# Six gate blocks of the last branch computed in pairs with seven products, and up products as the filler of the forgetting attention

## The chip, the cores and the metric

The kernel runs on one core of a Trainium2 chip. The metric is the device time of one execution in microseconds (us). Before the change the median of three runs is 2095.1 us (2092.2 to 2098.84).

## The reference, cut to what matters

One decoder layer in float32 on a sequence of 1024 tokens with 1024 channels. Its first part, the token mixers, is the one that the change touches:

```python
p = x @ w_in                                   # 1024 x 1024 times 1024 x (mixers + 4*1024 gates)
u_rw  = rwkv7_branch(...) @ rw_up              # each branch: 1024 x 256 times 256 x 1024
u_cv  = conv_branch(...)  @ cv_up
u_gla = gla_branch(...)   @ gla_up
u_fox = fox_branch(...)   @ fox_up             # forgetting attention, 4 heads of 64
gates = sigmoid(p_gate.reshape(B, T, 4, D) + gate_b)
merged = gates[0]*u_rw + gates[1]*u_cv + gates[2]*u_gla + gates[3]*u_fox
x = layer_norm(ALPHA * x + merged @ w_out)     # then cross-attention and a SwiGLU FFN
```

The gates are 4 x 1024 columns of `w_in`, so 32 blocks of 128 columns, 8 for each branch. All values are kept to float32 accuracy.

## The kernel before, in words

Activations lie transposed, channels on the 128 partitions and tokens along the free axis, in two halves of 512 tokens. To keep float32 accuracy every operand is split into a high and a low part (`split`, L161 a cast on ScalarE, L162 a subtraction on VectorE), and one product of 128 channels is three matmuls of 128x128 by 128x512: high times high (L179), high times low (L182), low times high (L183). TensorE therefore does three matmuls for each 128-channel slice (`mm3`).

A block of 128 columns of `w_in` can be computed in two ways. `project` does it directly: two halves of tokens, 8 slices, 3 matmuls, so 48 matmuls a block and 96 for two. The class `Sevens` takes a pair of blocks and the two token halves as a 2x2 matrix of matrices and computes it with seven products of half the depth instead of eight (the Strassen-Winograd scheme): 7 x 4 x 3 = 84 matmuls for two blocks. Its price is sums of weight quarters on GpSimd (`comb`, L389), seven pieces to split for a pair (ScalarE and VectorE), and sums of the outputs on VectorE (L379 to L382 and in `done`, L495).

The stages of the first part, with their places in the trace (us from the start of the span):

1. First projections, 30 to 262: the mixers' blocks. From 70 on they go through `Sevens`: two pairs of the RWKV branch and, from 112 on, eight pairs listed in `pairs0` (L409). `done` adds the last term, applies a sigmoid where one is due, and stores the block to DRAM (L506).
2. RWKV, 262 to about 610. `weave` alternates one step of the branch with pieces of a filler, here `gate_projections`: 16 gate blocks of branches 1 and 2 by `project`, cut in quarters of 6 matmuls, each half stored to `gate_d` in DRAM (L853).
3. Convolution and gated linear attention, then forgetting attention (`fox`, about 720 to 897). The filler is now `merge`: first `first_branch` (8 gate blocks of branch 0, kept on the chip, and its up products), then the 8 gate blocks of the last branch, with `other_branches` between them. `fox` has two head pairs, p = 0 and p = 1, each of 16 units of growing width (128 to 1024 columns, two units of each), and a step of it is followed by two pieces of filler (`FOX_PIECES`), each 6 matmuls whether it is a quarter of a gate block or an up product.
4. What is left of `merge` (`drain(pieces)`), 897 to 1006, and then the output projection.

One unit of `fox` is a chain over three engines: scores on TensorE (`ps_fs`), row maximum on VectorE (L1103, L1105, L1106), exponential on ScalarE (L1109), sum, reciprocal and scaling on VectorE (L1111 to L1113, `fp`), transposes on TensorE (`ps_ft`, L1120), a copy on ScalarE (`fpt`), and the products with the values on TensorE (`ps_fo`, L1133). Three units are in flight.

One up product in `other_branches` is 6 matmuls into `ps_up`, then a multiplication with the gate on VectorE (L1263, `gsig`, which also frees the PSUM bank), then an addition into `merged` on GpSimd (L1264). The gate's half is loaded from `gate_d` on the DMA queue of SyncE (L1252) into a ring of three tiles while the attention runs, and of nine afterwards. For each two up products 128x256 of weights are loaded and split (`uraw`, `uh`, `ul`), and for each branch its values (`yld`, `yh`, `yl`). The PSUM ring of up products and gate quarters has two banks.

Each engine takes its instructions in a fixed order. The order is made when the program is built: a scheduler places the instructions of the branch steps and of the filler, so the places in the code decide it only roughly.

Of the kernel before, what the change touches and what calls it, by code (L numbers as in the profile page):

```python
# [11 lines left out]
F32 = mybir.dt.float32  # L12
# [3 lines left out]
AF = mybir.ActivationFunctionType  # L16
# [6 lines left out]
P = 128  # L23
T = 1024
D = 1024
KD = D // P
# [11 lines left out]
ST_BLOCKS = ["cb0", "ca0", "cb1", "ca1", "gq", "gk", "gv0", "gv1", "gr0", "gr1",  # L38
             "fq0", "fk0", "fv0", "fq1", "fk1", "fv1"]
BLOCKS = RW_BLOCKS + ST_BLOCKS  # L40
# [52 lines left out]
def hybrid_kernel(ctx, tc, io, out):  # L93
    nc = tc.nc
# [4 lines left out]
    act = nc.scalar.activation  # L99
# [6 lines left out]
    stg = ctx.enter_context(tc.tile_pool(name="stg", bufs=3))  # L106
# [3 lines left out]
    dp = ctx.enter_context(tc.tile_pool(name="dp", bufs=1, space=DRAM))  # L110
# [25 lines left out]
    def pc(name, i=0):  # L136
        return par[:, PC[name] + i:PC[name] + i + 1]
# [54 lines left out]
    def drain(gen, n=None):  # L192

        while n is None or n > 0:
            if next(gen, gen) is gen:
                return
            n = n if n is None else n - 1
# [79 lines left out]
    def hs(hf):  # L277
        return slice(hf * TH, (hf + 1) * TH)
# [20 lines left out]
    def project(src, evac, w=None, pieces=1, both=True):  # L299

        wh, wl = w or weight(src)
        for hf in range(2):
            ps = gps("ps_g", both=both)
            pairs = [(wh[:, k * P:(k + 1) * P], wl[:, k * P:(k + 1) * P],
                      xh[k][:, hs(hf)], xl[k][:, hs(hf)]) for k in range(KD)]
            n = KD // pieces
            for i in range(pieces):
                mm3(ps, pairs[i * n:(i + 1) * n], i == 0, i == pieces - 1, lag=2 if pieces == 1 else 99)
                if i == pieces - 1:
                    evac(hf, ps)  # L310
                yield
# [29 lines left out]

    HK = KD // 2

    class Sevens:


# [59 lines left out]

    with ExitStack() as es:
        xtp = es.enter_context(tc.tile_pool(name="xtp", bufs=12))
        pairs0 = list(range(4, 8, 2)) + list(range(9, 9 + len(ST_BLOCKS), 2))  # L409

        def rows(u):
            pool, tag = (pM, "M") if u % 2 else (wp, "raw")
# [67 lines left out]
        for b in pairs0[0:2]:  # L480
            raws = [pM.tile([P, T], F32, tag="M", name="praw") for _ in range(2)]

            def done(i, l, a, ps):
                tt(out=raws[i][:, hs(l)], in0=a, in1=ps, op=ALU.add)
# [4 lines left out]
        for b in pairs0[2:]:  # L489
            held = {}  # L490

            def done(i, l, a, ps):
                n = BLOCKS[b + i]
                t = pM.tile([P, TH], F32, tag="M", name="stg2")
                tt(out=t, in0=a, in1=ps, op=ALU.add)  # L495
                if n[0] == "c":
                    if n[1] == "b":
                        act(t, t, AF.Sigmoid)
                    held.setdefault(l, []).append(t)
                    if len(held[l]) < 2:  # L500
                        return
                    tt(out=t, in0=t, in1=held[l][0], op=ALU.mult)
                    n = "cu" + n[2]
                elif n[:2] == "fq":
                    act(t, t, AF.Copy, scale=0.125)
                nc.sync.dma_start(st_d[n][:, hs(l)], t)  # L506

            sv.seven(rhs0, bank0, term, done)
        for k in range(HK):
            t = pM.tile([P, TH], F32, tag="M", name="x12")  # L510
# [333 lines left out]
        drain(fill)  # L844


    gate_d = dp.tile([24, P, T], F32, tag="gate_d", name="gate_d")

    def gate_block(i, pool, tag):
        def evac(hf, ps):  # L850
            t = pool.tile([P, TH], F32, tag=tag, name="gsig")
            act(t, ps, AF.Sigmoid, bias=pc("gateb", 8 + i))
            nc.sync.dma_start(gate_d[i, :, hs(hf)], t)  # L853

        return project(io["wblk"][len(BLOCKS) + 8 + i], evac, pieces=4, both=False)
# [335 lines left out]
    def values(br, t2):  # L1191

        yh, yl = [], []
        for k in range(2):
            h = t2.tile([P, T], F32R, tag="yh", name="yh", bufs=2)
            l = t2.tile([P, T], F32R, tag="yl", name="yl", bufs=2)
            for hf in range(2):
                t = t2.tile([P, TH], F32, tag="yld", name="yld")
                nc.sync.dma_start(t, y_d[br][k, :, hs(hf)])
                split(h[:, hs(hf)], l[:, hs(hf)], t)  # L1200
            yh.append(h)
            yl.append(l)
        return yh, yl

    def up_weights(br, j, t2):
        raw = t2.tile([P, 256], F32, tag="uraw", name="uraw")
        nc.sync.dma_start(raw, io["ups"][br, j])
        uh = t2.tile([P, 256], F32R, tag="uh", name="uh")
        ul = t2.tile([P, 256], F32R, tag="ul", name="ul")
        split(uh, ul, raw)  # L1210
        return uh, ul
# [26 lines left out]
    def other_branches(t2):  # L1238

        for br in (1, 2, 3):  # L1240
            while br not in ready:
                yield None
            y = values(br, t2)
            us, todo, sgs = [up_weights(br, 0, t2)], [(j, hf) for j in range(KD) for hf in range(2)], []

            def ahead(n):
                while len(sgs) < min(n, len(todo)):
                    j, hf = todo[len(sgs)]
                    late = 3 in ready
                    t = (pB if late else t2).tile([P, TH], F32, tag="B" if late else "sg", name="gsig",  # L1250
                                                  bufs=9 if late else 3)
                    nc.sync.dma_start(t, gate_d[8 * br + j - 8, :, hs(hf)])  # L1252
                    sgs.append(t)

            ahead(2)
            yield None
            for n, (j, hf) in enumerate(todo):
                if hf == 0 and j + 1 < KD:
                    us.append(up_weights(br, j + 1, t2))
                pu = gps("ps_up", both=False)  # L1260
                up_product(pu, us[j], y, hf)
                sg, mj = sgs[n], merged[j][:, hs(hf)]
                tt(out=sg, in0=sg, in1=pu, op=ALU.mult)  # L1263
                nc.gpsimd.tensor_tensor(out=mj, in0=mj, in1=sg, op=ALU.add)  # L1264
                ahead(n + (5 if 3 in ready else 3))
                yield True

    def merge(t2):
        yield from first_branch(t2)
        others = other_branches(t2)  # L1270
        for j in range(KD):
            yield from gate_block(16 + j, stg, "stg")
            for _ in range(10 if 3 in ready else 4):
                if next(others, None) is None:
                    break
                yield
        while True:
            r = next(others, others)
            if r is others:
                return  # L1280
            yield

    ready = {0}
    with ExitStack() as es:
# [569 lines left out]
    for f in reversed(range(LEAD)):  # L1854
        g = lead_up(f, 1, w13[f] if f > 1 else ffn_weights(f), (2, 2))
# [8 lines left out]
    for k in range(HK):  # L1864
        t = diff(x2[k + HK][:, hs(0)], xt[0].h[k + HK].bitcast(F32))
# [203 lines left out]
```

## Time and profile before

| what | us |
|---|---|
| median of three runs (lowest, highest) | 2095.1 (2092.2, 2098.84) |
| the profiled execution, its own time | 2095.68 |
| its span, first to last instruction | 2093.9 |
| first projections through `Sevens`, from the third pair on | 112 to 262 |
| forgetting attention, second head pair (p = 1) | 811 to 897 |
| rest of the merge | 897 to 1006 |

The page gives for each engine its busy time. TensorE is busy for 98% of the span and the chain of work that ended last runs over it for 88%. A matmul of 128x512 shows as 389 ns, but matmuls overlap: a new one starts every 0.226 to 0.227 us, so the count of matmuls in a stretch tells more than their busy time. What costs time besides the number of matmuls is a stretch in which the matmuls start further apart, because TensorE's next one waits for another engine.

### The profile page before, as it was taken

The page shows a single profiled execution, that of the slowest core. Times are in us where ns is not written, and L with a number is a line of the kernel's source. Part 1 is how long each engine was busy: PE and PEld are TensorE (multiplying, and loading weights), DVE is VectorE, ACT ScalarE, POOL GpSimd, SP SyncE. Part 2 cuts the span into 40 slices and gives each one's busy share as a digit, 9 for nine tenths or more (in the row PEclk, how much of TensorE's full clock was granted, in tenths as well). Part 3 has the DMA queues.
Part 4 walks back from the last instruction along what each step waited for, and adds up shares of the span by engine and source line. Part 5 has one row for each costly group of instructions (what it writes and reads, how often), then busy time and mean ns, then how long its engine had stood idle before and what let it go on. Part 6 is the DMA issues. An engine that isn't in the chain of part 4 may idle for free.

```text
span 2093.9 us, 29285 instructions
## 1 busy us (share of the span) xinstructions
PE 2050.9 (98%) x11404; PEld 1673.4 (80%) x11404; DVE 1292.9 (62%) x2237; ACT 768.0 (37%) x1320; POOL 431.9 (21%) x324
## 2 busy tenths in 40 slices
PE   8999999999999999999999999999999999999997
PEld 6888877877777877778788888877888888888877
DVE  8865456398624554654677345677666666666666
ACT  4332254222247567522244233453232222322331
POOL 4332200000000000244124000147131111222343
PEclk9999999999999999999999999999999999999998
DMA  5223242232223203354543102321311211211112
GB/s 169 72 86 106 97 142 87 74 91 68 69 96 99 78 30 121 98 193 139 170 150 124 44 31 81 110 102 41 101 41 41 81 41 41 71 51 41 56 46 81
DMA packets 100506, 181.08 MB, mean 86 GB/s; under 512 B 21030, under 2 KB 45400, under 8 KB 100368
## 3 DMA queue, kind: packets, MB, share of 16 engines
q1 hardware_dynamic: 100368, 179.21, 26.6%
q8 instruction: 90, 1.47, 0.3%
q14 instruction: 48, 0.39, 0.1%
HBM read 141.84 MB, written 37.34 MB: 86 GB/s over the span
## 4 chain that ended last, share of the span: by engine, by line
PE 88%; DVE 3%; POOL 3%; DMA 2%; ACT 2%; issue 2%; SPq 0%; DVEq 0%; POOLq 0%; ACTq 0%
PE ps_w L183 9%; PE ps_w L182 9%; PE ps_w L179 9%; PE ps_g L179 8%; PE ps_g L183 8%; PE ps_g L182 8%; PE ps_q L182 3%; PE ps_q L183 3%; PE ps_q L179 2%; PE ps_gate L179 1%; PE ps_wo L182 1%; PE ps_wo L183 1%; PE ps_wo L179 1%; PE ps_gate L183 1%; PE ps_up L179 1%
## 5 line engine op out<-in xcount | busy, mean ns | idle before, releaser
L182 PE MATMUL ps_g<-xh,wlo 128*128 128x512 f32 x464 | 184.5, 398 | 2.7 <-DVE wlo L162 2.7
L183 PE MATMUL ps_g<-xl,whi 128*128 128x512 f32 x464 | 184.9, 398 | 0.0
L179 PE MATMUL ps_g<-xh,whi 128*128 128x512 f32 x464 | 160.1, 417 | 2.2 <-ACT xh L161 2.2
L161 ACT CAST piece<-wraw 128x512 fp32r<-128x512 f32 x132 | 81.2, 622 | 199.7 <-PE ps_w L183 159.8
L183 PE MATMUL ps_w<-hid,piece 128*128 128x512 f32 (+1 forms) x400 | 143.3, 366 | 2.3 <-DVE hid L162 2.3
L161 ACT CAST piece<-wcomb 128x512 fp32r<-128x512 f32 x112 | 68.5, 621 | 209.5 <-PE ps_w L183 133.4
L182 PE MATMUL ps_w<-hid,piece 128*128 128x512 f32 (+1 forms) x400 | 143.2, 365 | 0.0
L162 DVE TENSOR_TENSOR wlo<-wraw,whi 128x1024 fp32r<-128x1024 f32 x79 | 98.4, 1249 | 58.5 <-ACT whi L161 58.3
L389 POOL TENSOR_TENSOR wcomb<-wraw,wcomb 128x512 f32<-128x512 f32 x28 | 40.8, 1458 | 398.7 <-DVE piece L162 397.7
L1788 DVE TENSOR_TENSOR x<-x,ps_w 128x512 f32<-128x512 f32 x120 | 82.5, 688 | 65.3 <-PE ps_w L183 65.3
L161 ACT CAST whi<-wraw 128x1024 fp32r<-128x1024 f32 x97 | 100.8, 1048 | 57.8 <-issue 18.4
L162 DVE TENSOR_TENSOR piece<-wraw,piece 128x512 fp32r<-128x512 f32 x124 | 96.7, 782 | 34.8 <-ACT piece L161 34.1
L162 POOL TENSOR_TENSOR wlo<-wraw,whi 128x1024 fp32r<-128x1024 f32 x18 | 46.6, 2594 | 321.3 <-ACT whi L161 311.4
L183 PE MATMUL ps_w<-xT,piece 128*128 128x512 f32 x288 | 112.0, 389 | 0.0
L182 PE MATMUL ps_w<-xT,piece 128*128 128x512 f32 x288 | 112.0, 389 | 0.0
L179 PE MATMUL ps_w<-hid,piece 128*128 128x512 f32 (+1 forms) x400 | 108.5, 366 | 0.2 <-DVE x L1786 0.2
L182 PEld LDWEIGHTS ps_g<-xh,wlo 128*128 128x128 f32 x464 | 88.6, 191 | 22.7 <-DVE wlo L162 3.1
L183 PEld LDWEIGHTS ps_g<-xl,whi 128*128 128x128 f32 x464 | 88.7, 191 | 19.8 <-issue 0.8
L179 PEld LDWEIGHTS ps_g<-xh,whi 128*128 128x128 f32 x464 | 83.4, 192 | 25.9 <-ACT xh L161 4.7
L389 POOL TENSOR_TENSOR wcomb<-wraw 128x512 f32<-128x512 f32 x58 | 78.4, 1352 | 101.2 <-DMA wraw<-ffn_w 46.8
L1264 POOL TENSOR_TENSOR merged<-merged,gsig 128x512 f32<-128x512 f32 x48 | 70.0, 1484 | 141.2 <-DVE gsig L1263 89.3
L162 DVE TENSOR_TENSOR piece<-wcomb,piece 128x512 fp32r<-128x512 f32 x112 | 87.3, 786 | 11.0 <-ACT piece L161 10.4
(528 smaller groups left out, 5234.9 us busy)
## 6 DMA issues: line engine op xcount, KB each, us to landing
wraw<-ffn_w SPq DMA_DIRECT2D x72, 512.0 KB
wraw<-wblk SPq DMA_DIRECT2D x57, 512.0 KB
gate_d<-gsig SPq DMA_DIRECT2D x48, 256.0 KB
gsig<-gate_d SPq DMA_DIRECT2D x48, 256.0 KB
wraw<-xa_wo SPq DMA_DIRECT2D x16, 512.0 KB
xraw<-xT SPq DMA_DIRECT2D x16, 256.0 KB
yld<-y_d SPq DMA_DIRECT2D x16, 256.0 KB
uraw<-ups SPq DMA_DIRECT2D x32, 128.0 KB
```

Source lines behind the costliest of these rows:

```text
L161: nc.scalar.copy(hi, src)
L162: eng.tensor_tensor(out=lo, in0=src, in1=hi.bitcast(F32), op=ALU.subtract)
L179: mm(ps, lhsT=pairs[i][0], rhs=pairs[i][2], start=start and i == 0, stop=False)
L182: mm(ps, lhsT=ll, rhs=rh, start=False, stop=False)
L183: latest[0] = mm(ps, lhsT=lh, rhs=rl, start=False, stop=stop and i == n + min(lag, n) - 1)
L389: nc.gpsimd.tensor_tensor(out=t, in0=a, in1=b, op=op)
L1264: nc.gpsimd.tensor_tensor(out=mj, in0=mj, in1=sg, op=ALU.add)
L1788: tt(out=xs, in0=xs, in1=ps, op=ALU.add)
```

## The change

Three edits, and one that follows from them.

- `pairs0` gets three more pairs: the first 6 of the 8 gate blocks of the last branch (`EARLY = 6`) are computed as pairs in the first projections. `done` adds the bias and the sigmoid for them and stores them to `gate_d`, whose allocation moves up for that.
- `merge` no longer interleaves 8 gate blocks with `other_branches`. It takes the steps of `other_branches` one after the other and, where that has nothing to give (it yields `None`) or the attention has ended (`3 in ready`), also a piece of `rest`, the last 2 gate blocks.
- `other_branches` yields `None` six times instead of once before the last branch's up products, and twice before those of the two others.

```diff
+    EARLY = 6
+    gate_d = dp.tile([24, P, T], F32, tag="gate_d", name="gate_d")
...
-        pairs0 = list(range(4, 8, 2)) + list(range(9, 9 + len(ST_BLOCKS), 2))
+        pairs0 = (list(range(4, 8, 2)) + list(range(9, 9 + len(ST_BLOCKS), 2))
+                  + list(range(len(BLOCKS) + 24, len(BLOCKS) + 24 + EARLY, 2)))
...
             def done(i, l, a, ps):
-                n = BLOCKS[b + i]
                 t = pM.tile([P, TH], F32, tag="M", name="stg2")
                 tt(out=t, in0=a, in1=ps, op=ALU.add)
+                g = b + i - len(BLOCKS)
+                if g >= 0:
+                    act(t, t, AF.Sigmoid, bias=pc("gateb", g))
+                    nc.sync.dma_start(gate_d[g - 8, :, hs(l)], t)
+                    return
+                n = BLOCKS[b + i]
...
             ahead(2)
-            yield None
+            for _ in range(6 if br == 3 else 2):
+                yield None
...
         others = other_branches(t2)
-        for j in range(KD):
-            yield from gate_block(16 + j, stg, "stg")
-            for _ in range(10 if 3 in ready else 4):
-                if next(others, None) is None:
-                    break
-                yield
+        rest = itertools.chain(*(gate_block(16 + j, stg, "stg") for j in range(EARLY, KD)))
         while True:
             r = next(others, others)
             if r is others:
-                return
-            yield
+                break
+            if r is None or 3 in ready:
+                if r:
+                    yield
+                next(rest, None)
+            yield
+        drain(rest)
```

How the instructions move is shown at two places, both in the forgetting attention at p = 1, at the units that are 768 columns wide. On TensorE, in the kernel before, the transposes of one unit, the scores of the next and what stands after them (`ps_g` is a gate block's bank):

```order
L1120 MATMUL ps_ft<-cst,fp 128x128 x6
L179 MATMUL ps_fs<-fkh,fqh 128x512
L182 MATMUL ps_fs<-fkh,fq 128x512
L183 MATMUL ps_fs<-fk,fqh 128x512
L179 MATMUL ps_fs<-fkh,fqh 128x256
L182 MATMUL ps_fs<-fkh,fq 128x256
L183 MATMUL ps_fs<-fk,fqh 128x256
L1099 LDWEIGHTS identb
L1099 MATMUL ps_fs<-lvl,identb 128x128
L179 MATMUL ps_g<-xh,whi 128x512 x2
L182 MATMUL ps_g<-xh,wlo 128x512
```

In the changed kernel the same place on TensorE (its line numbers are 9 higher here) reads:

```order
L1129 MATMUL ps_ft<-cst,fp 128x128 x6
L179 MATMUL ps_fs<-fkh,fqh 128x512
L182 MATMUL ps_fs<-fkh,fq 128x512
L183 MATMUL ps_fs<-fk,fqh 128x512
L179 MATMUL ps_fs<-fkh,fqh 128x256
L182 MATMUL ps_fs<-fkh,fq 128x256
L183 MATMUL ps_fs<-fk,fqh 128x256
L1108 LDWEIGHTS identb
L1108 MATMUL ps_fs<-lvl,identb 128x128
L179 MATMUL ps_up<-yh,uh 128x512 x2
L182 MATMUL ps_up<-yh,ul 128x512
```

The attention's own matmuls keep their order; the two pieces behind them, gate quarters before, are up products now. On VectorE, the kernel before has there, for one unit, maximum, sum, reciprocal and scaling with nothing between:

```order
L1103 TENSOR_REDUCE fst<-ps_fs 128x1 x2
L1105 TENSOR_TENSOR fst<-fst 128x1
L1106 TENSOR_SCALAR fst<-fst 128x1
L1111 TENSOR_TENSOR fst<-fst 128x1
L1112 RECIPROCAL fst<-fst 128x1
L1113 TENSOR_SCALAR fp<-fp,fst 128x768
```

and the changed kernel has on VectorE, for the same unit:

```order
L1112 TENSOR_REDUCE fst<-ps_fs 128x1 x2
L1114 TENSOR_TENSOR fst<-fst 128x1
L1115 TENSOR_SCALAR fst<-fst 128x1
L1273 TENSOR_TENSOR gsig<-gsig,ps_up 128x512
L1120 TENSOR_TENSOR fst<-fst 128x1
L1121 RECIPROCAL fst<-fst 128x1
L162 TENSOR_TENSOR ul<-uraw,uh 128x256
L1122 TENSOR_SCALAR fp<-fp,fst 128x768
L1273 TENSOR_TENSOR gsig<-gsig,ps_up 128x512
```

Two gate multiplications and one split of up weights have come in, one of each inside the unit's chain. At p = 1 the kernel before has 8 up products, the changed one all 32 of branches 1 and 2; behind the attention 40 before and 16 now.

## Rows read from the trace of the kernel before

**Rows 1.** Page, parts 1 and 4: busy time of each engine; shares of the last chain

```profile
PE 2050.9 (98%) x11404; PEld 1673.4 (80%) x11404; DVE 1292.9 (62%) x2237; ACT 768.0 (37%) x1320; POOL 431.9 (21%) x324
...
PE 88%; DVE 3%; POOL 3%; DMA 2%; ACT 2%; issue 2%; SPq 0%; DVEq 0%; POOLq 0%; ACTq 0%
```

**Rows 2.** Stretches (stretch, length, busy time and count of each engine, clock, DMA)

```profile
112.00:262.00 150.00, 150.00 (x662) 123.80 (x661) 82.89 (x116) 42.92 (x71) 41.77 (x35) 1.00 0.30 98
...
811.00:897.00 86.00, 83.61 (x514) 65.83 (x514) 46.06 (x110) 57.21 (x110) 10.70 (x8) 1.00 0.33 108
...
900.00:1010.00 110.00, 107.57 (x468) 86.63 (x467) 62.49 (x80) 33.49 (x58) 59.34 (x40) 1.00 0.55 179
```

**Rows 3.** Waits of TensorE, 810 to 900 (us in total, times, longest)

```profile
PE ps_ft L1120 <- DVE fp L1113: 2.4, 4, 0.9
```

**Rows 4.** Waits of TensorE, 900 to 1010

```profile
PE ps_up L179 <- DVE gsig L1263: 2.4, 2, 1.6
```

**Rows 5.** Timeline of TensorE at p = 1 (start, duration in us; idle before it)

```profile
813.74 0.23 PE L1099 MATMUL ps_fs<-lvl,identb 128*128 128x128 bf16 x1
...
836.11 0.23 PE L1099 MATMUL ps_fs<-lvl,identb 128*128 128x128 bf16 x1
...
847.05 0.66 PE L1120 MATMUL ps_ft<-cst,fp 128*128 128x128 f32 x4 [0.22 <-DVE fp L1113]
...
851.48 0.77 PE L1120 MATMUL ps_ft<-cst,fp 128*128 128x128 f32 x5 [0.36 <-DVE fp L1113]
...
877.06 0.95 PE L1120 MATMUL ps_ft<-cst,fp 128*128 128x128 f32 x7 [0.87 <-DVE fp L1113]
...
883.67 0.96 PE L1120 MATMUL ps_ft<-cst,fp 128*128 128x128 f32 x7 [0.93 <-DVE fp L1113]
```

**Rows 6.** Timeline of ScalarE at p = 1

```profile
869.74 1.28 ACT L852 ACT_TABLE_LOAD   x1
...
871.74 1.28 ACT L1109 ACT_TABLE_LOAD   x1
```

**Rows 7.** Timeline of VectorE, forgetting attention and the merge behind it

```profile
848.16 0.94 DVE L1105 TENSOR_TENSOR fst<-fst 128x1 f32<-128x1 f32 x1
...
874.85 1.46 DVE L162 TENSOR_TENSOR ul<-uraw,uh 128x256 fp32r<-128x256 f32 x1
...
877.90 1.21 DVE L162 TENSOR_TENSOR wlo<-wraw,whi 128x1024 fp32r<-128x1024 f32 x1
...
889.33 0.69 DVE L1103 TENSOR_REDUCE fst<-ps_fs 128x1 f32<-128x512 f32 x1 [0.84 <-PE ps_fs L1099]
...
892.31 0.75 DVE L1113 TENSOR_SCALAR fp<-fp,fst 128x1024 f32<-128x1024 f32 x1
...
972.81 0.42 DVE L162 TENSOR_TENSOR ul<-uraw,uh 128x256 fp32r<-128x256 f32 x1
```

**Rows 8.** Timeline of GpSimd, the same stretches

```profile
840.35 1.28 POOL L1264 TENSOR_TENSOR merged<-merged,gsig 128x512 f32<-128x512 f32 x1 [43.69 <-issue]
...
847.67 1.41 POOL L1264 TENSOR_TENSOR merged<-merged,gsig 128x512 f32<-128x512 f32 x1 [0.96 <-DVE gsig L1263]
...
874.75 1.28 POOL L1264 TENSOR_TENSOR merged<-merged,gsig 128x512 f32<-128x512 f32 x1 [1.77 <-DVE fst L1111]
...
971.63 13.63 POOL L1264 TENSOR_TENSOR merged<-merged,gsig 128x512 f32<-128x512 f32 x10 [9.56 <-DVE gsig L1263]
```

**Rows 9.** Timeline of SyncE's queue: DMA issues

```profile
841.66 0.32 SPq L1252 DMA_DIRECT2D gsig<-gate_d  x1
...
915.16 0.32 SPq L1199 DMA_DIRECT2D yld<-y_d  x1
```

**Rows 10.** Timeline of ScalarE: first use of a 256 KB load

```profile
918.96 0.62 ACT L161 CAST yh<-yld 128x512 fp32r<-128x512 f32 x1 [4.86 <-DMA yld<-y_d]
```

**Rows 11.** All instructions on the tile `gsig` (shortest/median/longest ns, first and last start)

```profile
L1263 DVE TENSOR_TENSOR gsig<-gsig,ps_up x48: 671/686/690, 839.5 to 1005.0; 128x512 f32<-128x512 f32 x48
L1264 POOL TENSOR_TENSOR merged<-merged,gsig x48: 1272/1410/2273, 840.4 to 1006.2; 128x512 f32<-128x512 f32 x48
```

More of the change, by code (lines that the diff above doesn't have):

```diff
@@ L844, in rwkv @@
         drain(fill)
-    gate_d = dp.tile([24, P, T], F32, tag="gate_d", name="gate_d")
     def gate_block(i, pool, tag):
```

## The prediction

> **What bounds the kernel now.** I read the page first. TensorE is busy for 98% of the span and carries 88% of the last chain [rows 1], so only two things move the time: how many matmuls there are, and where the next one comes late. The table of stretches gives the price of a matmul. From 112 to 262, the pairs with seven products, 662 matmuls fill 150 us: 0.2266 us each, at the full clock, with VectorE at 83 us, ScalarE at 43 and GpSimd at 42 of the 150 [rows 2]. No other engine is near its limit there. From 811 to 897, the second head pair of the forgetting attention, small matmuls mix with large ones and the count says less; the waits say that TensorE stood 2.4 us in four places for the scaled probabilities `fp` [rows 3]. From 900 to 1010, the rest of the merge, 468 matmuls take 110 us where 468 x 0.2266 = 106.05 would do: 3.95 us are lost, 2.4 of them to up products that wait for their bank, which VectorE frees [rows 2, 4]. So the change is read from three places: the number of matmuls, the stalls at p = 1, and the stalls behind the attention.
>
> **Term 1, the matmuls.** Six gate blocks cost 6 x 48 = 288 matmuls as they are. As three pairs they cost 3 x 84 = 252. The 36 that go are worth 36 x 0.2266 = 8.16 us. The 252 are added to the first projections, which get 57.1 us longer; the 288 leave the attention and the merge behind it. What a pair costs elsewhere (seven splits, four sums of weights, seven additions of outputs, here two sigmoids and two stores more) is hidden under its 84 x 0.2266 = 19.0 us of TensorE: the eight pairs of the row kept VectorE at 55% and the others under 30%. I put all that at nothing. If the cover failed, the next engine is VectorE, at 83/8 = 10.4 us a pair, so there are 8 us of room. Term 1: -8.2.
>
> **Term 2, the attention at p = 1.** 24 up products replace as many gate quarters, at the same six matmuls, and the two head pairs' own work stays. What changes is the company. An up product needs VectorE for 0.69 us [rows 11] and GpSimd for 1.3 to 1.4, its weights need a split for each two, and its gate has to come from DRAM; a gate quarter needed a sigmoid for each four and a large weight split now and then.
>
> First the ring of three gate tiles. A tile is loaded, multiplied, added, and only then loaded again: SyncE issued the next load 0.03 us after the addition that began at 840.35 and took 1.28 [rows 8, 9]. How long a 256 KB load takes is seen where ScalarE waited for one: issued at 915.16, used at 918.96, 3.8 us [rows 9, 10]. The loop is 3.8 + 0.69 + 1.4 = 5.9 us for three up products, 3.9 for the two of a unit. The first six units took (836.11 - 813.74) / 6 = 3.73 us each [rows 5]; at 3.9 they lose 6 x 0.2 = 1.2 us. Later units are longer and the ring is not their limit.
>
> Then the chain of a wide unit. In the widest, the maximum of the last half began at 889.33 and the scaling ended at 892.31 + 0.75 = 893.06: 3.8 us from scores to `fp` with the hand-overs, nothing of the filler between [rows 7]. Under it lie the two pieces behind the scores, 12 x 0.2266 = 2.7 us, and at least five matmuls of the next unit's scores, 1.1, at every other unit the longer products with the values: 3.8 us or more. So it fits now by a hair. The new order puts a gate multiplication and a split of up weights inside it. The multiplication falls into the time of the exponential; the split does not, and adds 0.42 us when GpSimd is idle, up to 1.46 when it is not [rows 7]. The chain becomes 4.2 to 5.3 us, so a stall of 0 to 1.5 us a unit; I take 0.5, since every other unit has the longer cover, for the ten units from 512 columns up: 5.0 us.
>
> These 5.0 are all the stalls of the new order, so the 2.4 of before go off in full. Three quarters of them sat beside gate work. The 0.87 at 877.06 followed an exponential that waited for a sigmoid with two loads of the activation table, 1.28 us each; the 0.93 at 883.67 followed a weight split of 1.21 us [rows 5 to 7]. With the gate blocks both causes go.
>
> Term 2: 1.2 + 5.0 - 2.4 = +3.8. Its ends: -2.4, if the unit's chain stays hidden everywhere. On the other side, all eight up products of before at 2.4 us together are 0.30 each, and 24 more at that price +7.2; still higher only if the ring or VectorE decides (below). I take the middle, since the stalls' causes are half removed and half multiplied.
>
> A rule of the Trainium skill speaks against the change here. At 874.85 a split of up weights, 0.42 us elsewhere, lasted 1.46 while GpSimd added from 874.75 to 876.03, and a one-column operation at 848.16 took 0.94 under an addition that began at 847.67; the gate multiplication, which reads one operand from PSUM, never took more than 0.69 [rows 7, 8, 11]. "SBUF — State Buffer", section "Who interferes with whom", says why: a VectorE instruction with two SBUF inputs, or in a two-port mode, contends with a GpSimd instruction that reads SBUF, and the one that comes second waits it out; the trace agrees on all three. At p = 1 GpSimd would now be busy 32 x 1.35 = 43 of 86 us. By that rule an affected operation waits with a chance of one half, 0.7 us on average, so 0.35; narrow units have about one of them, wide ones four: 8 x 0.35 + 8 x 1.4 = 14 us. If all of it reached TensorE, Term 2 would be 14 - 2.4 = +11.6 and the sum +1. That is the first rival.
>
> **Term 3, behind the attention.** 40 up products with 3.95 us of stalls become 16, all of the last branch, at 0.10 each 1.6: -2.4. The run of ten from 971 on kept the pace, GpSimd 13.63 us for ten [rows 8], so it may be -4.0; at worst nothing is gained. New is that the last branch's values are read back right after they are stored. A store and a load of 3.8 us each, 0.62 for the cast [rows 10] and 0.7 for the subtraction are 8.9 us, and eight gate quarters of 1.36 us, 10.9, stand in front. I put this at nothing; if the queue holds the loads back it costs 2 to 3 us.
>
> **The sum.** -8.2 + 3.8 - 2.4 = -6.8 us on the profiled execution's own 2095.7, so 2088.9. That execution lies 0.6 above the median of the runs, 2095.1, so I predict 2088.5. A measurement of this kernel can tell about 0.3%, 6.3 us, from no change; the forecast sits just beyond that line.
>
> **Rivals.** First, the gain is given back in the attention: the chain of a unit, with GpSimd's additions in VectorE's way, costs 9 to 14 us, and the time is 2091 to 2097. For it: the chain has no room now, and all four stalls sat within 10 us of up products. Against it: two of the four had a cause that goes, and VectorE's sum at p = 1 (46 us, plus 24 x 0.69 and 12 splits of 0.42 to 1.46, so 68 to 80) is still under the stretch's 86 [rows 2]. Chance 0.36.
>
> Second, the ring of three decides, and the kernel gets slower. In before its three tiles were always full when a group of up products began, so no row shows it in steady use. If a load, held behind others in SyncE's fixed order, comes back only so late that the loop takes 8.4 us, a unit takes 5.6 where the mean is 86 / 20 = 4.3: 16 x 1.3 = 21 us, and 2095.1 - 8.2 - 2.4 - 2.4 + 21 = 2103. It decides from a loop of about 8 us, a third above what the rows add up to. Chance 0.14.
>
> Third, the change doesn't save what it says because the longer first projections run into another engine; by [rows 2] it would need 19 us a pair where 10.4 are used. Chance 0.03, at 2095.
>
> **How the numbers follow.** The forecast, with Term 2 between -2.4 and +6, holds 0.47: from 2095.1 - 8.2 - 2.4 - 4.0 = 2080.5 to 2090.5. Most of it lies past the line and some of it doesn't; the rivals with 2091 to 2097 are within it; part of the second is beyond on the other side. Faster 0.45, same 0.41, slower 0.14. For 8 in 10 the range runs from 2082 to 2101.
>
> **What would show it.** The matmul count falls by 36, the first projections end 57 us later at 0.2266 a matmul, and TensorE shows no wait there. At p = 1 TensorE's wait for `fp` and for `gsig` together is some 6 us instead of 2.4, and no activation table is loaded between its exponentials. Behind the attention the stretch loses 1 to 2 us. I am wrong if the attention's second half grows by 8 us or more, and the cause is the ring if VectorE's gate multiplication waits for DMA, the shared port if GpSimd's additions and long splits stand before the stalls.

## The result, and the profile after

| | median, us | lowest, highest | profiled execution, its span |
|---|---|---|---|
| before (runs beside the changed kernel) | 2095.55 | 2092.2, 2098.84 | 2095.68, 2093.9 |
| after | 2112.59 | 2110.72, 2114.36 | 2110.72, 2108.9 |

The ratio is 1.0077, 95% interval [1.0061, 1.0093]: slower by 16 us by the ratio, 17 by the medians, where 2088.5 was forecast and the range ended at 2101.

The span grew by 15.0 us. I cut both traces at the same five places: the first product of the RWKV branch, the start and the last product of the second head pair (p = 1), and a place in the output projection up to which all that moved is done. Stretches of before (stretch, length, busy time and count of each engine, granted clock, DMA share, GB/s):

```profile
112.00:261.50 149.50, 149.50 (x661) 123.54 (x659) 82.39 (x116) 42.92 (x71) 41.77 (x35) 1.00 0.29 97
261.50:811.40 549.90, 545.77 (x4233) 425.43 (x4232) 319.01 (x714) 244.84 (x418) 16.62 (x20) 0.98 0.28 85
811.40:897.90 86.50, 84.11 (x523) 66.24 (x522) 45.76 (x110) 56.85 (x110) 10.70 (x8) 1.00 0.33 106
897.90:1052.00 154.10, 151.67 (x662) 123.12 (x663) 82.90 (x108) 37.96 (x63) 59.34 (x40) 1.00 0.52 169
1052.00:2093.90 1041.90, 1013.49 (x4900) 850.76 (x4898) 668.86 (x1076) 339.19 (x586) 256.95 (x188) 0.99 0.21 69
```

The same stretches of after, which answer to [rows 2]:

```profile
112.00:318.20 206.20, 206.20 (x911) 170.53 (x909) 112.88 (x158) 64.70 (x107) 57.35 (x47) 1.00 0.32 104
318.20:865.00 546.80, 544.04 (x4232) 424.21 (x4232) 318.51 (x713) 244.91 (x419) 16.82 (x20) 0.98 0.27 84
865.00:968.10 103.10, 90.02 (x523) 68.85 (x522) 79.57 (x149) 40.87 (x105) 43.52 (x32) 0.95 0.42 135
968.10:1064.00 95.90, 88.54 (x375) 70.67 (x375) 48.66 (x64) 23.72 (x37) 23.44 (x16) 0.98 0.47 157
1064.00:2108.90 1044.90, 1016.18 (x4899) 853.69 (x4897) 669.44 (x1076) 339.06 (x586) 256.27 (x188) 0.99 0.21 69
```

Row by row: the first projections take 56.7 us more and keep 0.2263 us a matmul. Up to p = 1 3.1 us less pass, at the same count. p = 1, with 523 matmuls as before, takes 16.6 us more, its clock 0.95, GpSimd at 43.5 us for 10.7. Behind the attention 287 matmuls fewer are worth 65.0 us, but only 58.2 are gone, so 6.8 are lost: 375 x 0.2266 = 85.0 of 95.9, 10.9 idle or slow, where before lost 154.1 - 662 x 0.2266 = 4.1. The rest, untouched, took 3.0 more; in the runs below that I cut there (up to 18 matmuls, 4 us, apart) it took 1038.5 to 1045.3 us whatever was changed, so I explain nothing by it.

TensorE's waits at p = 1, for [rows 3] (us in total, times, longest):

```profile
PE ps_ft L1129 <- DVE fp L1122: 10.6, 15, 1.5
PE ps_up L179 <- ACT yh L161: 1.2, 1, 1.2
PE ps_up L179 <- ACT gsig L861: 0.8, 1, 0.8
PE ps_g L179 <- DVE gsig L1273: 0.3, 1, 0.3
```

15 of the 16 units wait for their scaled probabilities, narrow ones too; before it was four. Why the scaling is late stands in the groups of VectorE for this stretch (count, busy time, mean ns, idle before):

```profile
L1273 DVE TENSOR_TENSOR gsig<-gsig,ps_up 128x512 f32<-128x512 f32 x32 | 21.9, 683 | 8.1 <-PE ps_up L183 8.1
L162 DVE TENSOR_TENSOR ul<-uraw,uh 128x256 fp32r<-128x256 f32 x17 | 16.4, 968 | 0.1
L1122 DVE TENSOR_SCALAR fp<-fp,fst 128x128 f32<-128x128 f32 (+7 forms) x16 | 12.2, 766 | 0.0
L1120 DVE TENSOR_TENSOR fst<-fst 128x1 f32<-128x1 f32 x8 | 5.9, 740 | 1.8 <-ACT fp L1118 1.7
L1115 DVE TENSOR_SCALAR fst<-fst 128x1 f32<-128x1 f32 x16 | 2.5, 154 | 0.6
```

An addition of one column against one column (L1120) took 0.74 us in the mean; its neighbour L1115, one column and a constant, 0.15. L1114, of the same form as L1120 but earlier in the order, ahead of the gate multiplication that lets an addition start, took 0.16: the form is held only where an addition runs beside it. By width the scaling is uneven too: at 384, 512 and 640 columns it took 0.92, 1.49 and 1.05 us, where it takes 0.41, 0.48 and 0.55 when GpSimd's additions are left out (below); at the other widths it took what it takes without them, and in the wider units the sum before it was held (1.12 and 1.21 us in the two of 896). The split of 128x256 up weights took 0.97, the multiplication with an operand in PSUM stayed at 0.68. The first row also answers for the ring of three gate tiles: what idle time stands before the multiplication is a wait for TensorE, and none for a load. One place in the timelines shows how the waits come about, the values of the second branch, where VectorE and GpSimd read:

```profile
907.43 0.67 DVE L162 TENSOR_TENSOR yl<-yld,yh 128x512 fp32r<-128x512 f32 x1
908.02 1.49 DVE L1122 TENSOR_SCALAR fp<-fp,fst 128x512 f32<-128x512 f32 x1
...
915.27 1.56 DVE L1122 TENSOR_SCALAR fp<-fp,fst 128x640 f32<-128x640 f32 x1
```

```profile
907.52 1.70 POOL L1274 TENSOR_TENSOR merged<-merged,gsig 128x512 f32<-128x512 f32 x1 [2.40 <-DVE fst L1121]
914.83 1.65 POOL L1274 TENSOR_TENSOR merged<-merged,gsig 128x512 f32<-128x512 f32 x1 [5.61 <-DVE gsig L1273]
```

and TensorE:

```profile
909.56 0.66 PE L1129 MATMUL ps_ft<-cst,fp 128*128 128x128 f32 x4 [1.50 <-DVE fp L1122]
911.46 0.80 PE L179 MATMUL ps_up<-yh,uh 128*128 128x512 f32 x1 [1.25 <-ACT yh L161]
912.06 0.63 PE L182 MATMUL ps_up<-yh,ul 128*128 128x512 f32 x1
912.48 0.63 PE L183 MATMUL ps_up<-yl,uh 128*128 128x512 f32 x1
...
920.61 0.39 PE L183 MATMUL ps_up<-yl,uh 128*128 128x512 f32 x1
920.84 0.40 PE L179 MATMUL ps_up<-yh,uh 128*128 128x512 f32 x1
```

Both scalings end some 0.3 us after the addition beside them has ended. After two stalls close together the matmuls start 0.43 apart, the lower of the clock's two levels (1.2 GHz), until about 920.3; the granted clock of that stretch is the 0.50 in its row:

```profile
911.40:920.30 8.90, 8.84 (x37) 7.02 (x38) 5.08 (x10) 3.39 (x10) 1.65 (x1) 0.50 0.45 156
```

So some 4 us are paid on top of the stalls (8.9 us at half the pace). An estimate for the whole of p = 1: the waits sum to 12.9 us for 2.4, and 103.1 us at a clock of 0.95 for 1.00 lose 5.2, together 15.7 of the 16.6. Of the causes I had seen in before, [rows 6], one activation table load is left at p = 1 instead of 14; the run of before with its additions on VectorE (below) shows that the loads had not been the cause.

### The profile page after: what moved, and what is told of

It is laid out like the page before. It is cut to its first block, busy times and chain, and to the rows that moved or that the text cites. A ratio compares the mean times of both kernels' runs of the same rounds, so it can differ in the third digit from the quotient of the medians.

```text
span 2108.9 us, 29333 instructions
## 1 busy us (share of the span) xinstructions
PE 2050.5 (97%) x11368; PEld 1671.8 (79%) x11368; DVE 1323.3 (63%) x2273; ACT 759.7 (36%) x1326; POOL 443.9 (21%) x336
## 4 chain that ended last, share of the span: by engine, by line
PE 84%; DVE 5%; POOL 3%; issue 3%; DMA 3%; ACT 3%; SPq 0%; DVEq 0%; POOLq 0%; ACTq 0%
PE ps_w L183 9%; PE ps_w L182 9%; PE ps_w L179 9%; PE ps_g L179 8%; PE ps_g L182 7%; PE ps_g L183 7%; PE ps_q L182 3%; PE ps_q L183 3%; PE ps_q L179 2%; PE ps_wo L183 1%; PE ps_wo L182 1%; PE ps_gate L179 1%; PE ps_wo L179 1%; PE ps_gate L183 1%; PE ps_gate L182 1%
## 5 line engine op out<-in xcount | busy, mean ns | idle before, releaser
L161 ACT CAST piece<-wcomb 128x512 fp32r<-128x512 f32 x124 | 75.9, 621 | 229.4 <-PE ps_w L183 133.2
L182 PE MATMUL ps_g<-xh,wlo 128*128 128x512 f32 x368 | 146.5, 398 | 4.2 <-DVE wlo L162 4.2
L183 PE MATMUL ps_g<-xl,whi 128*128 128x512 f32 x368 | 146.1, 397 | 0.0
L162 DVE TENSOR_TENSOR piece<-wraw,piece 128x512 fp32r<-128x512 f32 x133 | 104.5, 788 | 40.4 <-ACT piece L161 39.6
L179 PE MATMUL ps_g<-xh,whi 128*128 128x512 f32 x368 | 128.4, 418 | 1.2 <-ACT xh L161 0.8
L162 DVE TENSOR_TENSOR wlo<-wraw,whi 128x1024 fp32r<-128x1024 f32 x73 | 90.9, 1248 | 50.7 <-ACT whi L161 50.6
L393 POOL TENSOR_TENSOR wcomb<-wraw 128x512 f32<-128x512 f32 x64 | 86.8, 1358 | 113.7 <-DVE piece L162 80.3
L162 DVE TENSOR_TENSOR piece<-wcomb,piece 128x512 fp32r<-128x512 f32 x124 | 96.8, 787 | 11.2 <-ACT piece L161 10.5
L183 PEld LDWEIGHTS ps_w<-hid,piece 128*128 128x128 f32 x400 | 77.7, 194 | 14.7 <-DVE hid L162 2.7
L182 PEld LDWEIGHTS ps_w<-hid,piece 128*128 128x128 f32 x400 | 77.6, 194 | 12.1
L182 PEld LDWEIGHTS ps_g<-xh,wlo 128*128 128x128 f32 x368 | 70.2, 191 | 20.3 <-DVE wlo L162 4.6
```

What stands on the lines that cost most here:

```text
L161: nc.scalar.copy(hi, src)
L162: eng.tensor_tensor(out=lo, in0=src, in1=hi.bitcast(F32), op=ALU.subtract)
L179: mm(ps, lhsT=pairs[i][0], rhs=pairs[i][2], start=start and i == 0, stop=False)
L182: mm(ps, lhsT=ll, rhs=rh, start=False, stop=False)
L183: latest[0] = mm(ps, lhsT=lh, rhs=rl, start=False, stop=stop and i == n + min(lag, n) - 1)
L393: nc.gpsimd.tensor_tensor(out=t, in0=a, in1=b, op=op)
```

## The experiments

The kernel before, run beside each group of these, had medians of 2096.3 to 2097.6 us.

Theory 1: the additions on GpSimd hold VectorE's operations that read two SBUF tiles (and the scaling), and those stand in the chain of a unit. Rival A: VectorE simply has too much to do in its order. Rival B: the ring of three gate tiles. Theory T, behind the attention: the same hold, on the splits of the output weights and the merged sums.

**Which part of the change.** No block early, the new order alone:

```diff
-    EARLY = 6
+    EARLY = 0
...
-            ahead(2)
-            for _ in range(6 if br == 3 else 2):
+            for _ in range(24 if br == 3 else 2):
                 yield None
+            ahead(2)
...
-                next(rest, None)
+                drain(rest, 4 if r else 1)
```

> No gate block is made early (eight are made behind the forgetting attention again, as pieces between the last branch's up products), and the up products of the two middle branches fill the attention as in the changed kernel. Theory 1 (the up products as filler of the attention are what costs, by additions on GpSimd that hold VectorE up): the second pair of heads still takes 99 to 105 us, against 86.5 before and 103.1 after; the first projections are back at 149.5 us; the 36 matmuls x 0.2266 = 8.2 us come back, and the stretch behind the attention loses 2 to 5 us instead of 9 because gate pieces stand between its up products: 2109 to 2120 us. Rival (the early gate blocks cost elsewhere, the order of the attention is harmless): the attention at 86 to 90 us and 2094 to 2099.

Measured: 2113.8 us, ratio to before 1.0088 [1.0071, 1.0105]. The attention and the stretch behind it:

```profile
812.90:916.00 103.10, 90.04 (x523) 68.78 (x522) 79.52 (x149) 40.82 (x105) 43.50 (x32) 0.95 0.42 135
916.00:1069.00 153.00, 151.24 (x662) 123.67 (x662) 54.93 (x70) 37.98 (x55) 23.52 (x16) 1.00 0.43 140
```

The order alone costs all of the 16.6 us. And with gate pieces between them the last up products lose only 153.0 - 150.0 = 3.0 us, not 10.9.

**GpSimd's additions left out** (the sums of the two middle branches):

```diff
-                nc.gpsimd.tensor_tensor(out=mj, in0=mj, in1=sg, op=ALU.add)
+                if 3 in ready:
+                    nc.gpsimd.tensor_tensor(out=mj, in0=mj, in1=sg, op=ALU.add)
```

> The changed kernel without the GpSimd additions of the two middle branches to the merged sum (left out: those 32 sums; the products on VectorE, the loads and the matmuls stay). Theory 1 (GpSimd's additions hold VectorE's two-input operations): VectorE's low-part splits of the up weights fall from 0.97 us to 0.42, the 128x1 addition of the two row sums from 0.74 to 0.16, the scaling of the attention's rows to about 0.56 at 128x512; the second pair of heads takes 88 to 94 us instead of 103.1, and the kernel 2098 to 2104. Rival A (VectorE's own 62 us of work in its fixed order make the chain late): the waits for the scaling stay above 6 us, the stretch at 98 to 103 us, the kernel at 2107 to 2113. Rival B (three gate tiles): the loop gets shorter by one addition of 1.4 us, and VectorE's products would begin to wait for less; but since no product waits for a load in the trace, nothing.

Measured: 2093.7 us, p = 1 at 88.8 us; 14.3 of the 16.6 are gone, with every load, product and split still there. The same groups:

```profile
L1273 DVE TENSOR_TENSOR gsig<-gsig,ps_up 128x512 f32<-128x512 f32 x32 | 21.9, 685 | 7.0 <-PE ps_up L183 6.9
L1122 DVE TENSOR_SCALAR fp<-fp,fst 128x128 f32<-128x128 f32 (+7 forms) x16 | 8.2, 513 | 0.0
L162 DVE TENSOR_TENSOR ul<-uraw,uh 128x256 fp32r<-128x256 f32 x17 | 7.0, 417 | 0.0
L1120 DVE TENSOR_TENSOR fst<-fst 128x1 f32<-128x1 f32 x8 | 1.3, 159 | 2.1 <-ACT fp L1118 1.9
```

These three cost 4.0 + 9.4 + 4.6 = 18 us more under the additions; the wait for `fp` fell from 10.6 to 0.7. The kernel came out below my range: in the profiled execution the untouched rest took 1038.5 us, 6.4 less than in after, and why is not known.

**Taking single operations out of the hold.** The scaling on ScalarE:

```diff
-        tsc(out=pr[:, 0:n], in0=pr[:, 0:n], scalar1=st[:, 5:6], scalar2=None, op0=ALU.mult)
+        act(pr[:, 0:n], pr[:, 0:n], AF.Copy, scale=st[:, 5:6])
```

> The changed kernel with the scaling of the attention's rows (16 for each pair of heads) on ScalarE instead of VectorE; nothing is left out. Theory 1 (contention) and rival A (VectorE's queue) agree that VectorE is then 12 us emptier in the second pair of heads and that TensorE's waits for the scaling, 10.6 us, go to ScalarE's copy and shrink to 2 to 6 us: the stretch at 94 to 99 us, the kernel 2104 to 2109. If the row sums and the reciprocal, which stay on VectorE, are what is late, the wait only changes its name: 100 to 104 us and 2110 to 2114. If ScalarE's own order (exponentials, copies, rounded copies) makes it late, the first pair of heads gets longer too.

Measured: 2103.3 us, just below the forecast; p = 1 at 94.4, now with 531 matmuls in it. What held the scaling now holds the sum before it, and the split of the up weights hardly at all:

```profile
L162 DVE TENSOR_TENSOR ul<-uraw,uh 128x256 fp32r<-128x256 f32 x17 | 8.4, 491 | 0.0
L1120 DVE TENSOR_TENSOR fst<-fst 128x1 f32<-128x1 f32 x8 | 7.1, 886 | 1.9 <-ACT fp L1118 1.8
```

Then that sum with one tile and a scalar operand as well (`tsc(out=st[:, 3:4], in0=st[:, 3:4], scalar1=st[:, 4:5], ...)`):

> As the run with the scaling on ScalarE (2103.3 us), and the addition of the two row sums, which took VectorE 0.89 us there instead of 0.16, as an operation of one tile and a scalar operand from the tile (the 128x1 negation of the same form never took more than 0.15 us in any trace); nothing is left out. Theory 1 (GpSimd holds only some forms of VectorE's operations): the eight sums take 0.16 us each, 5.8 us less of VectorE, and TensorE's waits for the scaling fall from 4.9 us to 1 to 3: the second pair of heads at 90 to 93 us, the kernel 2099 to 2102. Rival A (VectorE's queue as such): the sum still waits for its turn; 94 us, 2102 to 2105.

Measured: 2097.8 us, again just below the forecast; p = 1 at 90.5 with 532 matmuls, the wait for `fp` 0.6.

```profile
L162 DVE TENSOR_TENSOR ul<-uraw,uh 128x256 fp32r<-128x256 f32 x17 | 15.2, 894 | 0.3
L1120 DVE TENSOR_SCALAR fst<-fst 128x1 f32<-128x1 f32 x8 | 1.7, 213 | 2.1 <-ACT fp L1118 2.0
```

The split of the up weights is held again, 0.89 us, and it hardly matters: the unit's chain passes VectorE in other instructions. Against their times with the additions left out, split and sum were held for 1.4 + 5.8 = 7.2 us in the run before this one and the split alone for 8.2 here, and still p = 1 fell from 94.4 to 90.5. So it is where the hold falls, not its total, that TensorE sees.

The low-part splits of the middle branches' up weights left out (the matmuls take the rounded weights in their place):

```diff
+        if br in (1, 2):
+            nc.scalar.copy(uh, raw)
+            return uh, uh
         split(uh, ul, raw)
```

> The changed kernel without the low part of the up weights of the two middle branches (left out: 16 subtractions on VectorE, 16.4 us in the second pair of heads; the matmuls take the rounded weights in the low part's place). Rival A (VectorE's work in its order): 16 us less of it takes the stretch from 103.1 to 91 to 96 us, the kernel to 2101 to 2106. Theory 1 (contention): GpSimd's additions then meet the tiny sums, the scaling and the values' splits in the subtractions' place; the stretch 96 to 101 us, the kernel 2106 to 2111.

Measured: 2107.3 us, p = 1 at 100.2: as theory 1 said, the additions meet the next operation in line:

```profile
L1122 DVE TENSOR_SCALAR fp<-fp,fst 128x128 f32<-128x128 f32 (+7 forms) x16 | 14.3, 892 | 0.3
```

Rival A had 91 to 96 us for p = 1. These splits took 14.6 us less, VectorE's sum fell by 9.2 (79.6 to 70.4, since scalings and sums took longer), and the stretch by 2.9.

**The additions on VectorE.** Shown for those of the middle branches; then, with the two engines exchanged, for those of the last branch; then for all:

```diff
-                nc.gpsimd.tensor_tensor(out=mj, in0=mj, in1=sg, op=ALU.add)
+                eng = nc.gpsimd if 3 in ready else nc.vector
+                eng.tensor_tensor(out=mj, in0=mj, in1=sg, op=ALU.add)
```

> The changed kernel with the 32 additions of the two middle branches on VectorE instead of GpSimd; nothing is left out. Theory 1 (the price is GpSimd's hold, not the amount of VectorE's work): the split of the up weights is back at 0.42 us, the sums at 0.16; VectorE gains 32 x 0.69 = 22 us of work and loses the 18 us of holding, so is as busy as before (about 83 of the stretch), but nothing in its chain waits in the middle for another engine: the second pair of heads at 92 to 98 us, 2102 to 2108. Rival A (the amount of VectorE's work in its order): 103 us or longer, 2111 to 2118.

Measured: 2095.9 us, ratio to before 0.9997 [0.9988, 1.0006], p = 1 at 89.8. Better than I expected: VectorE's sum, 77.5 us, is near the 79.6 of after, since an addition takes half of what GpSimd needs and nothing is held. So rival A falls here: nearly the same work, 13.3 us less at p = 1.

```profile
L1275 DVE TENSOR_TENSOR merged<-merged,gsig 128x512 f32<-128x512 f32 x32 | 21.8, 682 | 0.3
L162 DVE TENSOR_TENSOR ul<-uraw,uh 128x256 fp32r<-128x256 f32 x17 | 7.0, 413 | 0.0
```

> The changed kernel with the additions of the last branch (behind the attention) on VectorE instead of GpSimd; nothing is left out. Theory T (the stretch behind the attention loses its 7 us because GpSimd's 1.4 us additions hold the splits of the output weights and the products, and the splits of the merged sums wait for them): from the last attention product to the first output product 39 to 41 us instead of 44.0, the kernel 2107 to 2110. Rival (the loads of the output weights and the six-matmul products themselves make it late; VectorE is full): 44 to 46 us and 2112 to 2115.

Measured: 2104.6 us, 2.4 below the forecast. Up to the same place in the output projection:

```profile
967.50:1058.00 90.50, 89.41 (x381) 70.39 (x382) 53.13 (x81) 24.73 (x38) 0.00 (x0) 1.00 0.51 166
```

381 x 0.2266 = 86.3, so 4.2 us are lost instead of 10.9. In after this stretch had such rows on VectorE, each split beside an addition of GpSimd that it needs or meets:

```profile
996.60 1.95 DVE L162 TENSOR_TENSOR wlo<-wraw,whi 128x1024 fp32r<-128x1024 f32 x1 [0.94 <-ACT whi L161]
...
1006.42 1.76 DVE L162 TENSOR_TENSOR mA<-merged,mA 128x512 fp32r<-128x512 f32 x1 [0.59 <-POOL merged L1274]
```

with 1.22 and 0.68 us when GpSimd is idle, and TensorE's waits for [rows 4]:

```profile
PE ps_up L179 <- DVE gsig L1273: 4.5, 3, 1.8
PE ps_wo L179 <- ACT mA L161: 1.9, 1, 1.9
```

With the additions on VectorE the first are 0.8 and the second is gone.

> The changed kernel with all 48 additions to the merged sum on VectorE, GpSimd idle in both stretches; nothing is left out. Theory 1: the two savings measured apart (32 middle additions, 2112.6 to 2095.9; 16 last ones, 2112.6 to 2104.6) lie in different stretches and add up: 16.7 + 8.0 = 24.7, so 2088 us (2086 to 2091), faster than the kernel before by 6 to 10 us: the second pair of heads at 89 to 91 us, 31 to 33 us to the first output product. Rival (both remove one and the same loss, or the last branch's additions meet a VectorE that is now late from the attention): 2094 to 2098.

Measured: 2089.9 us, ratio to before 0.9957 [0.9945, 0.9969]: the two savings add up, and this version beats both kernels, the changed one by 22.7 us (medians of different groups) and before, run beside it, by 7.7. Its attention and what follows:

```profile
868.70:956.60 87.90, 84.93 (x523) 66.29 (x523) 77.34 (x181) 41.05 (x106) 0.00 (x0) 1.00 0.53 163
956.60:1047.80 91.20, 90.19 (x387) 71.58 (x387) 54.23 (x82) 25.05 (x38) 0.00 (x0) 1.00 0.50 161
```

With 387 x 0.2266 = 87.7 of 91.2, 3.5 us are lost. The ring is still of three; rival B falls.

> As the changed kernel with all additions on VectorE, and the scaling of the attention's rows on ScalarE as well, the two row sums in the one-input form; nothing is left out. Theory 1: with GpSimd idle TensorE waits only 0.8 us for the scaling, so taking 8 us more off VectorE gains 0 to 2 us: 2086 to 2090. Rival A (VectorE's amount of work, 77 us of 90 in the second pair of heads): 3 to 4 us more are gained, the stretch at 86 us, the kernel at 2084 to 2086.

Measured: 2091.2 us, ratio to before 0.9967 [0.9956, 0.9979]. No gain, and rival A's 2084 to 2086 is out: p = 1 took 91.1 us, with nine matmuls (2.0 us) more in it than in the run before, though VectorE's sum fell from 77.3 to 71.0. The scaling went to ScalarE, whose sum rose from 41.1 to 51.6, so what less work on VectorE alone would give is not shown.

**Was it the additions all along?** The kernel before with all additions on VectorE:

> The kernel before with all its additions to the merged sum on VectorE; nothing is left out. Theory 1: the order of before meets GpSimd's additions rarely at a place that TensorE waits for (2.4 us for the scaling, 2.4 us for the products behind the attention, some 2 us at half clock or unexplained), so at most 3 to 5 us are there to be had: 2091 to 2095. If it gains as much as the changed kernel does (20 us and more), the additions and not the order of the change were the trouble all along. If VectorE, with 33 us more to do, is late in the first output products: no change, 2095 to 2098.

Measured: 2098.0 us, ratio 1.0001 [0.9992, 1.001]. p = 1 fell by 1.5 us to 85.0, and the stretch behind it, where VectorE got 40 additions, took 155.8 at 663 matmuls, 1.7 more: I had hoped for 3 to 5. So in the order of before the additions cost little, and the move gave nothing in sum; why it cost behind the attention is open.

But p = 1 shows more than its 1.5 us:

```profile
810.40:895.40 85.00, 84.99 (x524) 66.66 (x523) 46.20 (x118) 56.79 (x110) 0.00 (x0) 1.00 0.34 109
```

TensorE waits for nothing there, and not once for `fp`, with all 14 table loads and the splits of the gate weights still in place. So the four stalls of before, [rows 3], were the additions' hold as well. The one at 877.06 followed the split of [rows 7] that lasted 1.46 us; before the one at 883.67 the trace of before has on VectorE, and on GpSimd beside it:

```profile
880.54 0.90 DVE L162 TENSOR_TENSOR ul<-uraw,uh 128x256 fp32r<-128x256 f32 x1
881.56 1.05 DVE L1111 TENSOR_TENSOR fst<-fst 128x1 f32<-128x1 f32 x1
...
879.86 2.73 POOL L1264 TENSOR_TENSOR merged<-merged,gsig 128x512 f32<-128x512 f32 x2 [3.83 <-DVE fst L1106]
```

The sum of one unit, 0.16 us elsewhere, ended at 882.61, when the additions had ended at 882.59, and its scaling began at 882.84.

**Is the saving of 36 matmuls real?** The new order without early blocks, with the additions on VectorE:

> The reordered kernel without early gate blocks, with all additions on VectorE; nothing is left out. Term 1 of the forecast (36 matmuls fewer, 8.2 us) was in the first projections but the reordered kernel with early gates was only 1.2 us below the one without. Theory 1 (the saving is real and was eaten behind the attention, where the gate pieces that stood between the last up products were gone and GpSimd's additions held VectorE): with GpSimd idle the saving shows: 6 to 9 us above the run with all additions on VectorE and early gates, 2094 to 2097. Rival (the early blocks cost as much elsewhere as they save): within 2 us of that run.

Measured: 2096.5 us, ratio to before 0.9996 [0.9986, 1.0007]: above the kernel with early blocks by 6.6 us by the medians and 8.2 by the two ratios. Yes, for 8.16 worked out. With the additions on GpSimd only 1 to 2 us of it showed (2113.8 against 2112.6, ratios 1.0088 and 1.0077): the last up products, without the gate pieces, lost 10.9 - 3.0 = 7.9 us more.

**A smaller dose.** Two early blocks, and the order of before:

```diff
-    EARLY = 6
+    EARLY = 2
...
+        for j in range(EARLY, KD):
+            yield from gate_block(16 + j, stg, "stg")
+            for _ in range(10 if 3 in ready else 4):
```

> The kernel before with two gate blocks of the last branch made early, and the order of the attention's filler as it was (eight gate pieces, then four up products). Theory 1: 12 matmuls x 0.2266 = 2.7 us are saved, the second pair of heads stays at 86 to 87 us since it keeps gate pieces as filler; the stretch behind it has 96 gate matmuls less beside 40 up products, of which it gives back 0 to 2 us: 1 to 3 us faster than before. If early gate blocks cost elsewhere (a colder start behind the first projections, more DMA): no change or slower by 1 to 2 us.

Measured: 2109.5 us, ratio 1.0056 [1.0043, 1.007], so 13 us slower where I expected 1 to 3 faster.

```profile
825.40:911.90 86.50, 84.10 (x523) 66.30 (x522) 45.77 (x110) 56.86 (x110) 10.71 (x8) 1.00 0.32 106
911.90:1062.00 150.10, 135.97 (x566) 108.05 (x567) 81.44 (x106) 33.34 (x57) 59.00 (x40) 0.95 0.50 160
```

The attention is that of before to the tenth of a microsecond. Behind it 566 matmuls, 128.3 us, took 150.1: two gate blocks fewer among 40 up products, and 21.8 us are lost instead of 4.1. TensorE waited 5.7 us once for a branch's values, whose loads stood behind others on SyncE, with the matmuls 0.43 apart after it, 5.8 us for multiplications, as in after, and 2.5 for a split of the merged sums; and its clock in this stretch was 0.95. So in this one run the price of thinner filler was far from linear. How it splits between loads and the hold was not tried.

## Why the prediction was wrong

- **Term 1 was right**: 56.7 us more in the first projections for 57.1 worked out, no wait in them, and 6.6 to 8.2 us of saving for the 8.16 were measured between two kernels with the additions on VectorE that differ in whether the blocks are made early or stand behind the attention.
- **Term 2 was mis-sized, and decided**: +3.8 forecast, +16.6 measured. The step that failed is "I take 0.5" for the ten wide units: I priced the new chain by the one split inside it. The runs showed that the hold falls on the chain's own links as well, the scaling (0.77 us for 0.51) and the sum of the row's halves (0.74 for 0.16), and in the narrow units too. The half clock after the branch's values was not in the sum at all. The line "With the gate blocks both causes go" failed as well: the two stalls that it put down to table loads and a weight split were the same hold (the run of before with its additions on VectorE has the loads and the splits, and no such stall), so the new order did not take their cause away but brought 32 additions for 8.
- **The rule I had weighed was right, its price too low, and my argument against it wrong.** The Trainium skill, "SBUF — State Buffer", section "Who interferes with whom", names two SBUF inputs as a case that contends and `tensor_scalar`, the scaling's form, as one that can enter a two-port mode and contend, and spares the reduction and an instruction with at most one SBUF input outside such a mode. The trace of after agrees: the split (0.97 us), the sum (0.74) and the scaling (0.77) were held, the reduction of 512 columns (0.69) and the multiplication with its operand in PSUM (0.68) were not; in which mode the scaling ran, no run shows by itself. The run without additions gives 14.3 us to the hold, where the rival allowed 9 to 14. I gave it 0.36 for two reasons. That two of four stalls had a cause that goes was the misreading above. That VectorE's sum of 68 to 80 us was "still under the stretch's 86" proves nothing for a chain in which VectorE's turn comes twice a unit: it was 79.6.
- **The ring of three** (1.2 of Term 2, and the slower rival) had no part in it: no multiplication waited for a load in the changed kernel. The rival on the slow side named the right sign with the wrong mechanism, and its 21 us came from 20 units in the stretch's 86 us where the rows count 16, 5.4 us each. (2095.1 - 6.8 is 2088.3, not 2088.5; nothing hangs on it.)
- **Term 3 had the wrong sign**: -2.4 forecast, +6.8 measured. The step that failed is "at 0.10 each": the mean over 40 up products with gate pieces between them was carried over to 16 with hardly any. The run of ten from 971 on that I relied on was one dense group with slack on either side; with the gate pieces in place the same 16 lose 3.0 us, without them 10.9.
- **The last branch's values** were in time, as put at nothing. The 3.1 us gained before p = 1 lie behind the first projections, where the granted clock of the first 55 to 59 us is 0.97 for 0.91. I had not foreseen them, and they are not reliable: that stretch took 544.5 to 549.7 us in the runs with early blocks that I cut there, 549.1 to 551.7 without.

## What to carry to other kernels

The filler of a latency-bound chain should leave alone the engines that the chain runs over: six matmuls of a gate block and six of an up product cost TensorE the same, but the first left GpSimd free and took little of VectorE (45.8 us in all of p = 1, for 79.6). Elementwise work on GpSimd beside such a chain is priced by the VectorE operations that it holds, here those that read two SBUF tiles, whatever their size, and the scaling; look for a tiny operation whose mean grew nearly fivefold. A stall's neighbour is not yet its cause: in before, the run that took the additions away settled it. Before work is taken out of a stretch, ask what it separates: the saving here came through only after the additions had moved.

## What the runs showed of the hardware

A VectorE addition of 128x1 took 0.16 us with GpSimd idle and, at the place in the order where GpSimd's additions met it, 0.74 to 0.89 in the mean, but 0.21 once its second operand was a scalar operand from the tile, as it does with GpSimd idle. The same 128x512 addition took 1.36 us on GpSimd and 0.68 on VectorE, so moving 32 of them to the busier engine left its busy time as it was (79.6 to 77.3 us).
